# A two-layer decoder trunk: seven products of sums for two of eight pairs of K tiles, with two of the four weight sums made by accumulating DMAs

## The chip, the cores and the metric

One core of a Trainium2 chip runs the whole program. The metric is the device time of one execution in microseconds (us). Engines are named as the profile names them: PE is TensorE (matmul; PEld its weight loads), DVE is VectorE, ACT is ScalarE, POOL is GpSimd, SP is SyncE, which here only issues DMAs. SPq, ACTq and POOLq are these engines as issuers of DMAs.

## What is computed

Two layers over 256 tokens of width 2048, in float32. Nearly all arithmetic is in products of the 256 x K activations with weight matrices:

```python
def swiglu(h, w_gate, w_up, w_down):
    return (jax.nn.silu(h @ w_gate) * (h @ w_up)) @ w_down      # 2048 -> 5632 -> 2048
...
def short_conv_mixer(h, w_in, conv_w, w_out):
    bg, cg, z = jnp.split(h @ w_in, 3, axis=-1)                 # 2048 -> 3 x 2048
    z = cg * z
    zc = lax.conv_general_dilated(z, conv_w[:, None, :], ...)   # depthwise, width 3
    return (bg * zc) @ w_out                                    # 2048 -> 2048
...
def reference(x, ...):
    h = x
    for i in range(DEPTH):                                      # 2
        hn = rmsnorm(h, norm_mix[i])
        if i % 2 == 0:
            mix = sgu_nsa_mixer(hn, ...)                        # 2048 -> 4632 columns, attention, 2048 -> 2048
        else:
            mix = short_conv_mixer(hn, ...)
        h = h + mix
        h = h + swiglu(rmsnorm(h, norm_ffn[i]), w_gate[i], w_up[i], w_down[i])
    return rmsnorm(h, norm_f)
```

## The kernel before

Every product of activations with a weight matrix goes through one object, `Stream`. A weight matrix is cut into strips of 512 columns (NW) and tiles of 128 rows (K tiles). `gemm` plans one strip: a load of four K tiles (1024 KB) at a time on SP's queue into `raw` (three buffers), and units of two K tiles. For a unit, `split` writes each weight as a rounded part `wh` (ScalarE, L82) and the rest `wl` (VectorE, L83), and `multiply` issues twelve matmuls: two K tiles, two halves of the tokens (m), and three products each, xh*wh, xh*wl and xl*wh (L99 to L101). The activations are split the same way into a high and a low part (`a_h`, `a_l` for the normed h, `t_h`, `t_l` for the hidden layer, `y`, `z_h`, `z_l`). One strip gathers in two PSUM banks of `psg` (pool of four).

The order is written out by hand: `run` takes unit after unit; after the matmuls of unit i it splits ahead (`ahead`: AHEAD = 3 units, with a ring of AHEAD + 1 pairs `wh`, `wl`), then calls what is due (`done` at a strip's last unit, and functions hung on later units by `at`). Each engine works its own queue in this order. A raw buffer is loaded again as soon as its last split is recorded.

The feed-forward layer does 11 pairs of strips, gate then up; after each pair g = silu(gate) * up is transposed on TensorE into `t_h`, `t_l`; then w_down in four strips of 44 K tiles, added to h (L276, `norm_from`). The convolution layer does for each of four strips cg, z and bg, and then w_out_c. The attention part of layer 0 (up to about 320 us) and w_out_ab use the same stream. At the start SP loads the first pieces of x (256 KB each) and the first weights in turn (end of `trunk`, L176 and L71).

Of the kernel before, what the change touches and what calls it, by code (L numbers as in the profile page):

```python
# [27 lines left out]
NEG = -1e30  # L28
AHEAD = 3
PROBS, VALUES = 4, 6  # L30


class Stream:


    def __init__(self, nc, raws, parts, psg):
        self.nc, self.raws, self.parts, self.psg = nc, raws, parts, psg
        self.raw_plan, self.units = [], []
        self.raw, self.hl = {}, {}
        self.loaded = self.split_to = 0  # L40
        self.hooks = {}
        self.at_unit = 0

    def gemm(self, w, groups, n0, src, done, tail=0, between=None):
# [3 lines left out]
        for gi, g in enumerate(groups):  # L48
            k0, gk = g if isinstance(g, tuple) else (g, 4)
            ri = len(self.raw_plan)  # L50
            self.raw_plan.append((w[k0 * P:(k0 + gk) * P, n0:n0 + NW].rearrange("(k p) n -> p k n", p=P), gk * NW))
            for j in range(gk // 2):
                self.units.append({
                    "raw": ri, "j": j, "k0": k0 + 2 * j, "src": src, "chunk": chunk, "free": j == gk // 2 - 1,
                    "first": gi == 0 and j == 0, "last": gi == len(groups) - 1 and j == gk // 2 - 1, "tail": 0,
                })
            if between and gi < len(groups) - 1:
                ap, use = between.pop(0)
                self.units.append({"raw": len(self.raw_plan), "j": 0, "use": use, "free": True})
                self.raw_plan.append((ap, 2 * NW))  # L60
        if tail:
            self.units[-tail]["tail"] = tail

# [11 lines left out]
    def split(self, pieces=(slice(0, 2),)):  # L75
        u = self.units[self.split_to]
        nc = self.nc
        src = self.raw[u["raw"]][:, 2 * u["j"]:2 * u["j"] + 2, :]
        hv = self.parts.tile([P, 2, NW], F32R, name="wh")
        lv = self.parts.tile([P, 2, NW], F32R, name="wl")  # L80
        for ks in pieces:
# [889 lines left out]
```

## Time and profile before

| | |
|---|---|
| median of 3 runs | 2187.59 us (2186.87 to 2188.07) |
| profiled execution | 2187.05 us, span 2185.3 us |
| TensorE busy | 2174.6 us |
| VectorE, ScalarE busy | 1149.6 us, 988.3 us |
| moved by DMA | 410.95 MB, mean 188 GB/s |
| granted clock | 0.999 of full speed |

The profile is that of one execution; busy time is the time in which an engine has an instruction, and for TensorE neighbouring matmuls overlap, so the mean of one record is more than the distance between two. The page gives shares over the whole span; stages differ, so the text below reads the feed-forward stage (500 to 1000 us, and again in the second layer) by itself.

### The profile page before, as it was taken

The page shows a single profiled execution, that of the slowest core. Times are in us where ns is not written, and L with a number is a line of the kernel's source. Part 1 is how long each engine was busy: PE and PEld are TensorE (multiplying, and loading weights), DVE is VectorE, ACT ScalarE, POOL GpSimd, SP SyncE. Part 2 cuts the span into 40 slices and gives each one's busy share as a digit, 9 for nine tenths or more (in the row PEclk, how much of TensorE's full clock was granted, in tenths as well). Part 3 has the DMA queues.
Part 4 walks back from the last instruction along what each step waited for, and adds up shares of the span by engine and source line. Part 5 has one row for each costly group of instructions (what it writes and reads, how often), then busy time and mean ns, then how long its engine had stood idle before and what let it go on. Part 6 is the DMA issues. An engine that isn't in the chain of part 4 may idle for free.

```text
span 2185.3 us, 24414 instructions
## 1 busy us (share of the span) xinstructions
PE 2174.6 (100%) x9900; PEld 1796.8 (82%) x9900; DVE 1149.6 (53%) x1269; ACT 988.3 (45%) x1178; POOL 28.3 (1%) x59
## 2 busy tenths in 40 slices
PE   9999999999999999999999999999999999999998
PEld 7887788888888888888888888888888888888886
DVE  6577655555444544544455555554554455444444
ACT  6456545444444444444444444444444444444443
POOL 2000000000000000000000000000000000000000
PEclk9999999999999999999999999999999999999999
DMA  7664455665555555555556555556555555556553
GB/s 261 204 198 134 136 176 190 193 193 183 188 190 191 192 191 188 188 187 190 192 184 201 185 182 191 190 187 192 192 193 191 188 186 186 192 193 197 197 193 135
DMA packets 214577, 410.95 MB, mean 188 GB/s; under 512 B 6744, under 2 KB 18448, under 8 KB 214464
## 3 DMA queue, kind: packets, MB, share of 16 engines
q1 hardware_dynamic: 210416, 404.52, 56.9%
q10 hardware_dynamic: 3664, 3.63, 0.5%
q8 instruction: 77, 1.26, 0.2%
q0 software_dynamic: 384, 1.25, 0.2%
q14 instruction: 36, 0.29, 0.0%
HBM read 407.27 MB, written 2.10 MB: 187 GB/s over the span
## 4 chain that ended last, share of the span: by engine, by line
PE 99%; issue 0%; DMA 0%; DVE 0%; SPq 0%; POOLq 0%; POOL 0%; ACT 0%; DVEq 0%
PE pg L99 32%; PE pg L101 32%; PE pg L100 32%; PE pm L227 2%; PE pm L537 0%; PE pm L614 0%; PE pm L403 0%; PE pm L570 0%; DMA h<-in_x_dram 0%; PE pm L501 0%; PE pm L688 0%; PE pm L617 0%; PE pm L577 0%; POOLq L966 0%; POOL nf_r L899 0%
## 5 line engine op out<-in xcount | busy, mean ns | idle before, releaser
L83 DVE TENSOR_TENSOR wl<-raw,wh 128x1024 fp32r<-128x1024 f32 (+1 forms) x769 | 939.1, 1224 | 923.0 <-ACT wh L82 920.4
L82 ACT ACTIVATE wh<-raw 128x1024 fp32r<-128x1024 f32 (+1 forms) x769 | 812.0, 1059 | 962.3 <-PE pg L101 952.7
L99 PE MATMUL pg<-wh,a_h 128*128 128x512 f32 x2080 | 820.6, 394 | 0.0
L101 PE MATMUL pg<-wh,a_l 128*128 128x512 f32 x2080 | 810.6, 390 | 0.0
L100 PE MATMUL pg<-wl,a_h 128*128 128x512 f32 x2080 | 810.0, 389 | 0.0
L101 PEld LDWEIGHTS pg<-wh,a_l 128*128 128x128 f32 x2080 | 390.7, 188 | 82.1
L100 PEld LDWEIGHTS pg<-wl,a_h 128*128 128x128 f32 x2080 | 391.0, 188 | 81.7 <-issue 2.2
L99 PEld LDWEIGHTS pg<-wh,a_h 128*128 128x128 f32 x2080 | 390.9, 188 | 81.4 <-issue 2.1
L99 PE MATMUL pg<-wh,t_h 128*128 128x512 f32 x704 | 274.3, 390 | 0.0
L101 PE MATMUL pg<-wh,t_l 128*128 128x512 f32 x704 | 273.9, 389 | 0.0
L100 PE MATMUL pg<-wl,t_h 128*128 128x512 f32 x704 | 273.9, 389 | 0.0
L101 PEld LDWEIGHTS pg<-wh,t_l 128*128 128x128 f32 x704 | 132.1, 188 | 27.4
L100 PEld LDWEIGHTS pg<-wl,t_h 128*128 128x128 f32 x704 | 132.2, 188 | 27.3
L99 PEld LDWEIGHTS pg<-wh,t_h 128*128 128x128 f32 x704 | 132.2, 188 | 27.3
L99 PE MATMUL pg<-wh,y 128*128 128x512 f32 x128 | 50.4, 394 | 0.0
L99 PE MATMUL pg<-wh,z_h 128*128 128x512 f32 x128 | 50.2, 392 | 0.0
L101 PE MATMUL pg<-wh,y 128*128 128x512 f32 x128 | 49.9, 390 | 0.0
L101 PE MATMUL pg<-wh,z_l 128*128 128x512 f32 x128 | 49.9, 390 | 0.0
L100 PE MATMUL pg<-wl,y 128*128 128x512 f32 x128 | 49.8, 389 | 0.0
L100 PE MATMUL pg<-wl,z_h 128*128 128x512 f32 x128 | 49.8, 389 | 0.0
L239 DVE TENSOR_TENSOR t_l<-pm,t_h 128x512 fp32r<-128x512 f32 x44 | 28.4, 686 | 32.4 <-ACT t_h L238 32.4
L238 ACT ACTIVATE t_h<-pm 128x512 fp32r<-128x512 f32 x44 | 23.9, 595 | 46.2 <-PE pm L227 46.2
(182 smaller groups left out, 780.3 us busy)
## 6 DMA issues: line engine op xcount, KB each, us to landing
raw<-in_w_gate_dram SPq DMA_DIRECT2D x88, 1024.0 KB, 5.2
raw<-in_w_up_dram SPq DMA_DIRECT2D x88, 1024.0 KB, 5.2
raw<-in_w_down_dram SPq DMA_DIRECT2D x88, 1024.0 KB, 5.1
raw<-in_w_in_c_dram SPq DMA_DIRECT2D x48, 1024.0 KB, 5.1
raw<-in_w_in_ab_dram SPq DMA_DIRECT2D x34, 1024.0 KB, 5.2
raw<-in_w_out_ab_dram SPq DMA_DIRECT2D x16, 1024.0 KB, 5.1
raw<-in_w_out_c_dram SPq DMA_DIRECT2D x16, 1024.0 KB, 5.1
raw<-in_w_in_ab_dram SPq DMA_DIRECT2D x4, 512.0 KB, 6.7
```

The costliest lines, as they stand in the source:

```text
L82: nc.scalar.activation(hv[:, ks], src[:, ks], AF.Copy)
L83: nc.vector.tensor_sub(lv[:, ks], src[:, ks], hv[:, ks].bitcast(F32))
L99: nc.tensor.matmul(ps[m], xh[:, kt, sl], hv[:, k, :], start=u["first"] and k == 0, stop=False)
L100: nc.tensor.matmul(ps[m], xh[:, kt, sl], lv[:, k, :], start=False, stop=False)
L101: nc.tensor.matmul(ps[m], xl[:, kt, sl], hv[:, k, :], start=False, stop=u["last"] and k == 1)
L227: nc.tensor.transpose(t[:, k * S + m * P:k * S + (m + 1) * P], src[:, m, c + k * P:c + (k + 1) * P], ident)
L238: nc.scalar.activation(dh[:, k0:k0 + 2, :], t, AF.Copy)
L239: nc.vector.tensor_sub(dl[:, k0:k0 + 2, :], t, dh[:, k0:k0 + 2, :].bitcast(F32))
```

## The change

The two strips that belong together (gate and up, two strips of w_down, cg and z, two of bg, two of w_out_c) become one `block`. In it a pair of K tiles and the two strips form a product of 2 x 2 tiles: tiles of x for two K tiles and two halves of the tokens, tiles of w for two K tiles and two strips. For most pairs it is done as before, in 8 products of three matmuls each, as units of kind n with twelve matmuls. For the pairs numbered 4 and 6 of eight (`SUMS`; of six pairs only number 4) it is done with seven products of sums of tiles: four differences of x tiles (`x_split`, lines L430 to L432 on VectorE), four sums of w tiles, and sums of the products (`summed`). These take four units of kind s: three with six matmuls, one with three. With a0, a1 the two K tiles of the first strip and b0, b1 of the second, the weight sums are a0 + b0 and b1 + b0 (loads of a0 and b1 into `ts`, and for each a DMA from GpSimd that adds b0 to it, L184), a0 + b0 + b1 and a0 + a1 + b0 + b1 (VectorE, L137 and L140). The strings N8, F8 and N6 set the order of the units: N8 is five n, then s and n mixed, then three n; F8 ends with two n, and so does N6 (six pairs). Four products keep banks of their own (`FREE`, from `psm`, which also serves the transposes); the other four banks (`BANK`) are those of `psg`, and gather ordinary products and three of the seven.

Loads are now of two K tiles (512 KB) into six buffers, eight from the end of w_out_ab on, and from there the ring of split weights has five places, so splits run four units ahead. The feed-forward layer is done in three parts of 4, 4 and 3 strips (`PARTS`): gate/up blocks of a part, then its part of w_down, added to h. The last two strips of w_down in layer 1 stay as they were. The attention part and w_out_ab are as before apart from the size of the loads. At the start SP sends two weight loads where it sent one.

```diff
+RAWS = 6
+MORE = 2
+TS = 2
+PARTS = (4, 4, 3)
+SUMS = {4: 0, 6: 1}
+BANK = ((1, 3), (2, 7))
+P1, P5, P6, P7 = FREE = (0, 4, 5, 6)
...
+    def widen(self, pool):
+
+        self.ring.insert(self.slot, (pool, len(self.ring)))
+        self.sums = pool
+        self.free += [pool] * MORE
...
+            item = queue[c].pop(0)
+            if c == "n":
+                item[1]["raw"] = self.plan(item[0])
+                u = item[1]
+            elif item:
+                wk, t, s = item
+                ts = []
+                ra, rb = self.plan(wk[0]), self.plan((wk, ts))
+                sums13 = None
+
+                def sum2(ra=ra, rb=rb, ts=ts):
+                    self.nc.vector.tensor_add(self.raw[rb][:, 0], ts[0][:, 0], self.raw[rb][:, 1])
+
+                def sum4(ra=ra, rb=rb, ts=ts):
+                    self.nc.vector.tensor_add(ts[0][:, 2], self.raw[rb][:, 0], self.raw[ra][:, 1])
+
+                sevens = [
+                    {"raw": ra, "prep": sums13, "mms": [(0, t(0, 0), P1), (1, t(1, 0), BANK[0][0])]},
+                    {"raw": rb, "ts": ts, "at": 0, "then": sum2, "mms": [(0, s(1), P5), (1, s(0), P7)]},
+                    {"raw": rb, "then": sum4, "frees": (ra,), "mms": [(0, s(2), P6), (1, s(3), BANK[1][0])]},
+                    {"raw": rb, "ts": ts, "at": 2, "w": 1, "mms": [(0, t(1, 1), BANK[0][1])]},
+                ]
+                u = sevens.pop(0)
+            else:
...
+        assert not queue["n"] and not queue["s"]
+        self.on(last_sum, lambda: summed(0, chunk["banks"]))
+        self.on(last_sum + 1, lambda: summed(1, chunk["banks"]))
+        end = len(self.units)
+        self.soon[end - 1] = lambda: done(0, chunk["banks"])
+        self.soon[end] = lambda: done(1, chunk["banks"])
+        for u, fn in begun:
+            self.on(first + u, fn)
...
     def load(self):
-        if self.loaded < len(self.raw_plan):
-            ap, n = self.raw_plan[self.loaded]
-            t = self.raws.tile([P, 4 * NW], F32, name="raw")
-            self.nc.sync.dma_start(out=t[:, :n].rearrange("p (k n) -> p k n", n=ap.shape[-1]), in_=ap)
-            self.raw[self.loaded] = t.rearrange("p (k n) -> p k n", n=NW)
+        while self.free and self.loaded < len(self.raw_plan):
+            ap = self.raw_plan[self.loaded]
+            pool = self.free.pop(0)
+            t = pool.tile([P, 2 * NW], F32, name="raw", bufs=RAWS if pool is self.raws else MORE)
+            v = t.rearrange("p (k n) -> p k n", n=NW)
+            if isinstance(ap, tuple):
+                (wa, wb), ts = ap
+                ts.append(self.sums.tile([P, 3, NW], F32, name="ts", bufs=TS))
+                self.nc.sync.dma_start(out=ts[0][:, 0], in_=wa[:, 0])
+                self.nc.sync.dma_start(out=ts[0][:, 1], in_=wb[:, 1])
+                for k in range(2):
+                    self.nc.gpsimd.dma_start(out=ts[0][:, k], in_=wb[:, 0], accum_op=ALU.add)
+                self.nc.sync.dma_start(out=v[:, 1], in_=wb[:, 1])
+            else:
+                self.nc.sync.dma_start(out=t.rearrange("p (k n) -> p k n", n=ap.shape[-1]), in_=ap)
+            self.raw[self.loaded] = v
+            self.home[self.loaded] = pool
             self.loaded += 1
...
+        for ks in pieces or (slice(0, w),):
             nc.scalar.activation(hv[:, ks], src[:, ks], AF.Copy)
+            if "then" in u:
+                u["then"]()
             nc.vector.tensor_sub(lv[:, ks], src[:, ks], hv[:, ks].bitcast(F32))
-        self.hl[self.split_to] = (hv, lv)
+        self.hl[i] = (hv, lv)
         self.split_to += 1
-        if u["free"]:
-            self.load()
+        if "frees" in u:
+            self.free.append(self.home[u["raw"]])
+            if u["frees"] != 1:
+                self.free.append(self.home[u["frees"][0]])
+        self.load()
...
+        c = u["chunk"]
+        if "mms" in u:
+            for x, (j, op, key) in enumerate(u["mms"]):
+                uses = c["uses"][key]
+                if uses[0] == (i, x):
+                    c["banks"][key] = self.bank(key)
+                ps = c["banks"][key]
+                xh, xl = op()
+                nc.tensor.matmul(ps, xh, hv[:, j, :], start=uses[0] == (i, x), stop=False)
+                nc.tensor.matmul(ps, xh, lv[:, j, :], start=False, stop=False)
+                nc.tensor.matmul(ps, xl, hv[:, j, :], start=False, stop=uses[-1] == (i, x))
+            return
...
-        while self.split_to < min(len(self.units), i + 1 + min(AHEAD, 2 + i // 8)):
+        while self.split_to < min(len(self.units), i + 1 + min(len(self.ring) - 1, 2 + i // 8)):
...
             self.multiply(i)
+            if i in self.soon:
+                self.soon[i]()
             self.ahead(i)
...
+    def x_split(src, dst, kp, gain=None):
+
+        ks = slice(2 * kp, 2 * kp + 2)
+        if kp not in SUMS:
+            split_T([src.rearrange("p (k m) c -> p k (m c)", k=2)], (dst.h, dst.l), 2 * kp, gain)
+            return
+        xs = late["pool"].tile([P, 8, P], F32, name="xs")
...
+        v = a.rearrange("p (k m) c -> p k (m c)", k=2)
+        nc.vector.tensor_sub(xs[:, 4:6], a[:, 0:2], a[:, 1:4:2])
+        nc.vector.tensor_sub(xs[:, 6], a[:, 0], xs[:, 5])
+        nc.vector.tensor_sub(xs[:, 7], a[:, 2], xs[:, 6])
+
+        def parts():
+            i = SUMS[kp]
+            nc.scalar.activation(dst.h[:, ks], v, AF.Copy)
+            nc.scalar.activation(dst.sh[:, i], xs[:, 4:], AF.Copy)
+            nc.vector.tensor_sub(dst.l[:, ks], v, dst.h[:, ks].bitcast(F32))
+            nc.vector.tensor_sub(dst.sl[:, i], xs[:, 4:], dst.sh[:, i].bitcast(F32))
+
+        st.at(1, parts)
...
+    def summed(part, b):
+
+        if part == 0:
+            g, u = (late["pool"].tile([P, MT, NW], F32, name=n) for n in ("ga", "ub"))
+            late["g"], late["u"] = g, u
+            nc.scalar.activation(g[:, 0], b[P1], AF.Copy)
+            return
+        g, u = late["g"], late["u"]
+        nc.vector.tensor_sub(u[:, 0], b[P6], g[:, 0])
+        nc.vector.tensor_sub(g[:, 1], b[P7], u[:, 0])
+        nc.vector.tensor_sub(u[:, 1], b[P5], g[:, 1])
+        nc.vector.tensor_add(u[:, 0], b[P5], u[:, 0])
...
+    def add_to_h(n2, squares=None):
+
+        c0 = 2 * n2 * NW
+
+        def sums(part, b):
+            summed(part, b)
+            if part:
+                for n, t in enumerate((late["g"], late["u"])):
+                    hs = h[:, :, c0 + n * NW:c0 + (n + 1) * NW]
+                    nc.vector.tensor_add(hs, hs, t)
+
+        def done(n, b):
+            for m in range(MT):
+                hs = h[:, m, c0 + n * NW:c0 + (n + 1) * NW]
+                nc.vector.tensor_add(hs, b[BANK[n][m]], hs)
+            if squares:
+                st.at(1, lambda: [squares(2 * n2 + n, m) for m in range(MT)])
+
+        return sums, done
...
+    N8 = [(k, k in SUMS) for k in range(8)], "nnnnn sns sns sns sns nnn"
+    F8 = [(k, k in (4, 6)) for k in range(8)], "nnnnnn sns sns sns sns nn"
+    N6 = [(k, k in SUMS) for k in range(6)], "nnn nn sn sn sn s nn"
...
+                st.block([(w_gate[layer], 0, c * NW), (w_up[layer], 0, c * NW)], F8 if c == 0 else N8, src_a, begun[:],
+                         summed, done)
+                begun[:] = [(2, lambda p=pairs: p(0)), (3, lambda p=pairs: p(1))]
+            last = part == len(PARTS) - 1
+            for n2 in range(2):
+                if last and layer == 1 and n2 == 1:
+                    break
+                sums, done = add_to_h(n2, norm[0] if last else None)
+                ws = [(w_down[layer], 4 * c0, 2 * n2 * NW), (w_down[layer], 4 * c0, (2 * n2 + 1) * NW)]
+                st.block(ws, N8 if nb == 4 else N6, src_x, begun[:], sums, done)
+                begun[:] = norm[1](n2) if last else []
+            c0 += nb
+
+    def then_pairs(pair, scale):
...
+    order = F8
+    for c in (0, 2):
+        for cc in (c, c + 1):
+            done, then = done_cz(cc)
+            st.block([(wc, 0, D + cc * NW), (wc, 0, 2 * D + cc * NW)], order, src_a, begun[:], summed, done)
+            begun[:] = then
+            order = N8
+        done, then = done_bg(c)
+        st.block([(wc, 0, c * NW), (wc, 0, (c + 1) * NW)], N8, src_a, begun[:], summed, done)
+        begun[:] = then
+    squares, pair, scale = norm_from("f1", g_ffn[1])
+    begin = then_pairs(pair, scale)
+    for n2 in range(2):
+        sums, done = add_to_h(n2, squares)
+        st.block([(w_out_c[0], 0, 2 * n2 * NW), (w_out_c[0], 0, (2 * n2 + 1) * NW)], N8 if n2 else F8, src_x, begun[:], sums,
+                 done)
+        begun[:] = begin(n2)
 
 
...
+    free = st.free
     for b in range(3):
+        st.free = free[:2]
         st.load()
```

How the order of instructions moves, at three places. The first is TensorE in a gate/up block. Before, half a unit, one of its two K tiles (with numbers: pg_5360 and pg_5361 are the banks of the two halves of the tokens):

```order
L99 MATMUL pg_5360<-wh_5335,a_h_79 128x512
L100 MATMUL pg_5360<-wl_5336,a_h_79 128x512
L101 MATMUL pg_5360<-wh_5335,a_l_80 128x512
L99 MATMUL pg_5361<-wh_5335,a_h_79 128x512
L100 MATMUL pg_5361<-wl_5336,a_h_79 128x512
L101 MATMUL pg_5361<-wh_5335,a_l_80 128x512
```

Now, the second and third unit of a pair done with sums (sa_h and sa_l are the split sums of x tiles, pm the banks of single products):

```order
L229 MATMUL pm_3767<-wh1_3703,sa_h_2717 128x512
L230 MATMUL pm_3767<-wl1_3704,sa_h_2717 128x512
L231 MATMUL pm_3767<-wh1_3703,sa_l_2718 128x512
L229 MATMUL pm_3771<-wh1_3703,sa_h_2717 128x512
L230 MATMUL pm_3771<-wl1_3704,sa_h_2717 128x512
L231 MATMUL pm_3771<-wh1_3703,sa_l_2718 128x512
L229 MATMUL pm_3779<-wh2_3727,sa_h_2717 128x512
L230 MATMUL pm_3779<-wl2_3728,sa_h_2717 128x512
L231 MATMUL pm_3779<-wh2_3727,sa_l_2718 128x512
L229 MATMUL pg_3646<-wh2_3727,sa_h_2717 128x512
L230 MATMUL pg_3646<-wl2_3728,sa_h_2717 128x512
L231 MATMUL pg_3646<-wh2_3727,sa_l_2718 128x512
```

A split weight now feeds one half of the tokens only, and a unit has six matmuls. Over the program the matmuls of 512 columns in these products are 237 fewer, and the transposes of activations number 368 in both.

The second place is SP's queue in the same blocks: the loads of weights. Before, four of a strip of gate, then four of up:

```order
L71 DMA raw<-in_w_in_ab_dram 128x4x512 x18
L71 DMA raw<-in_w_out_ab_dram 128x4x512 x16
L71 DMA raw<-in_w_gate_dram 128x4x512 x4
L71 DMA raw<-in_w_up_dram 128x4x512 x4
L71 DMA raw<-in_w_gate_dram 128x4x512 x4
```

Now, around the two summed pairs of a block (L181 and L182 load the two tiles of `ts` that GpSimd's DMAs of L184 add to, L185 the second tile of the second strip again):

```order
L187 DMA raw<-in_w_gate_dram 128x2x512 x2
L181 DMA ts<-in_w_gate_dram 128x512
L182 DMA ts<-in_w_up_dram 128x512
L185 DMA raw<-in_w_up_dram 128x512
L187 DMA raw<-in_w_up_dram 128x2x512
L187 DMA raw<-in_w_gate_dram 128x2x512 x2
```

A summed pair takes one load of 512 KB and three of 256 KB here, and two accumulations of 256 KB on GpSimd's queue. There the row scales (`r_f`, `r_c`) stand between accumulations.

The third place is VectorE at the end of a strip of w_down, where its sum goes into h. Before:

```order
L83 TENSOR_TENSOR wl<-raw,wh 128x1024 x21
L276 TENSOR_TENSOR h<-pg,h 128x512 x2
L83 TENSOR_TENSOR wl<-raw,wh 128x1024
L245 SCALAR_TENSOR_TENSOR a_l<-pm,gains,a_h 128x256 x4
L83 TENSOR_TENSOR wl<-raw,wh 128x1024 x21
```

Now, at the end of a block of w_down over six pairs, in layer 0 (ga and ub are the two buffers of product sums; the splits from wl_8689 on belong to the next block):

```order
L208 TENSOR_TENSOR wl_8689<-raw,wh_8688 128x1024
L472 TENSOR_TENSOR ub<-pm,ga 128x512
L473 TENSOR_TENSOR ga<-pm,ub 128x512
L474 TENSOR_TENSOR ub<-pm,ga 128x512
L475 TENSOR_TENSOR ub<-pm,ub 128x512
L503 TENSOR_TENSOR h<-h,ga 128x2x512
L503 TENSOR_TENSOR h<-h,ub 128x2x512
L208 TENSOR_TENSOR wl_8704<-raw,wh_8703 128x1024
L208 TENSOR_TENSOR wl_8722<-raw,wh_8721 128x1024
L508 TENSOR_TENSOR h<-pg,h 128x512 x2
L208 TENSOR_TENSOR wl_8742<-raw,wh_8741 128x1024
L508 TENSOR_TENSOR h<-pg,h 128x512 x2
```

The additions that empty the `pg` banks (L508) stand behind the six operations on product sums and behind three splits for the next block, whose first unit writes into the first of these banks.

## Rows read from the trace of the kernel before

**Rows 1.** The page: busy time, and the span in 40 slices (PE, granted clock, DMA).

```profile
PE 2174.6 (100%) x9900; PEld 1796.8 (82%) x9900; DVE 1149.6 (53%) x1269; ACT 988.3 (45%) x1178; POOL 28.3 (1%) x59
PE   9999999999999999999999999999999999999998
...
PEclk9999999999999999999999999999999999999999
DMA  7664455665555555555556555556555555556553
```

**Rows 2.** The page: the chain that ended last, by engine.

```profile
PE 99%; issue 0%; DMA 0%; DVE 0%; SPq 0%; POOLq 0%; POOL 0%; ACT 0%; DVEq 0%
```

**Rows 3.** Timeline, gate/up stretch of layer 0: start us, us, engine, line, operation [idle before].

```profile
699.83 0.39 PE L99 MATMUL pg<-wh,a_h 128*128 128x512 f32 x1
...
700.51 0.39 PE L99 MATMUL pg<-wh,a_h 128*128 128x512 f32 x1
...
701.39 1.06 ACT L82 ACTIVATE wh<-raw 128x1024 fp32r<-128x1024 f32 x1 [1.66 <-PE pg L101]
...
702.48 1.23 DVE L83 TENSOR_TENSOR wl<-raw,wh 128x1024 fp32r<-128x1024 f32 x1 [1.50 <-ACT wh L82]
...
704.11 1.06 ACT L82 ACTIVATE wh<-raw 128x1024 fp32r<-128x1024 f32 x1 [1.66 <-PE pg L101]
```

**Rows 4.** Chain in order of time: transposes after two successive gate/up pairs (start us, us).

```profile
492.79 0.87 PE pm L227 x8
537.23 0.87 PE pm L227 x8
```

**Rows 5.** Groups of instructions: count | busy us, mean ns of one | idle before.

```profile
L83 DVE TENSOR_TENSOR wl<-raw,wh 128x1024 fp32r<-128x1024 f32 (+1 forms) x769 | 939.1, 1224 | 923.0 <-ACT wh L82 920.4
L82 ACT ACTIVATE wh<-raw 128x1024 fp32r<-128x1024 f32 (+1 forms) x769 | 812.0, 1059 | 962.3 <-PE pg L101 952.7
L769 DVE SCALAR_TENSOR_TENSOR ga<-pg,r_f,ga 128x512 f32<-128x512 f32 x44 | 30.9, 743 | 0.0
L760 ACT ACTIVATE ga<-pg,r_f 128x512 f32<-128x512 f32 x44 | 30.0, 690 | 20.6 <-PE pg L101 20.6
L276 DVE TENSOR_TENSOR h<-pg,h 128x512 f32<-128x512 f32 x24 | 15.4, 682 | 0.0
```

**Rows 6.** Timeline of VectorE in the convolution layer: operations back to back.

```profile
1199.60 1.28 DVE L815 TENSOR_TENSOR cg<-pg,cg 128x512 f32<-128x512 f32 x2
1208.70 3.50 DVE L83 TENSOR_TENSOR wl<-raw,wh 128x1024 fp32r<-128x1024 f32 x3
```

**Rows 7.** Windows: us, busy of PE, PEld, DVE, ACT, POOL, clock, DMA share, GB/s.

```profile
5.00:20.00 15.00, 14.69 (x66) 11.92 (x66) 9.11 (x14) 10.25 (x21) 7.32 (x23) 1.00 1.06 375
500.00:1000.00 500.00, 500.00 (x2248) 414.83 (x2247) 248.27 (x225) 214.66 (x229) 0.00 (x0) 1.00 0.58 190
```

**Rows 8.** DMA issues: count, KB each, median us from issue to landing.

```profile
raw<-in_w_gate_dram SPq DMA_DIRECT2D x88, 1024.0 KB, 5.2
...
raw<-in_w_in_ab_dram SPq DMA_DIRECT2D x4, 512.0 KB, 6.7
...
h<-in_x_dram ACTq DMA_DIRECT2D x5, 256.0 KB, 5.4
nfg<-in_norm_f_dram POOLq DMA_DIRECT2D x4, 256.0 KB, 5.4
```

**Rows 9.** Start: SP's issues on the timeline, and the chain's first piece.

```profile
1.71 0.46 SPq L71 DMA_DIRECT2D raw<-in_w_in_ab_dram  x1
2.21 0.47 SPq L176 DMA_DIRECT2D h<-in_x_dram  x1
...
2.21 4.53 DMA h<-in_x_dram
```

More of the change, by code (lines that the diff above doesn't have):

```diff
@@ L49, in gemm @@
             k0, gk = g if isinstance(g, tuple) else (g, 4)
[L50 to L56, printed above, removed]
+            for k in range(k0, k0 + gk, 2):
+                ri = self.plan(w[k * P:(k + 2) * P, n0:n0 + NW].rearrange("(k p) n -> p k n", p=P))
+                self.units.append({"raw": ri, "k0": k, "src": src, "chunk": chunk, "frees": 1, "first": gi == 0 and k == k0,
+                                   "last": gi == len(groups) - 1 and k == k0 + gk - 2, "tail": 0})
@@ L73, in load, with split @@
             self.loaded += 1
-    def split(self, pieces=(slice(0, 2),)):
-        u = self.units[self.split_to]
+    def split(self, pieces=None):
+        i = self.split_to
+        u = self.units[i]
         nc = self.nc
[L78 to L81, printed above, removed]
+        if u.get("prep"):
+            u["prep"]()
+        w = u.get("w", 2)
+        src = u["ts"][0][:, u["at"]:u["at"] + w] if "ts" in u else self.raw[u["raw"]]
+        pool, k = self.ring[self.slot]
+        self.slot = (self.slot + 1) % len(self.ring)
+        hv = pool.tile([P, 2, NW], F32R, name=f"wh{k}")
+        lv = pool.tile([P, 2, NW], F32R, name=f"wl{k}")
+        for ks in pieces or (slice(0, w),):
@@ L123, in run @@
                 continue
-            if u["first"]:
-                c["ps"] = [self.psg.tile([P, NW], F32, name="pg") for _ in range(MT)]
-            if u["tail"]:
+            if u.get("first"):
+                c["ps"] = [self.bank(k) for k in BANK[self.turn]]
+                self.turn ^= 1
+            if u.get("tail"):
                 for j in range(i, i + u["tail"]):
@@ L266, in trunk @@
     R = {}
[L268 to L290 removed]
+    late = {}
@@ new lines, in x_pair, with open_late @@
+    def x_pair(src, c, dst, kp, gain=None):
+        t = transposed_bank(src, c).rearrange("p k (m c) -> p (k m) c", m=MT)
+        st.at(1, lambda: x_split(t, dst, kp, gain))
+    def open_late():
+        next_region()
+        pool = late["pool"] = region("late")
+        pool.tile([P, LATE_PAD], F32, name="pad")
+        for n in ("a", "x"):
+            for x in "hl":
+                late[n + x] = pool.tile([P, len(SUMS), 4, P], F32R, name=f"s{n}_{x}")
+        src_a.sh, src_a.sl = late["ah"], late["al"]
+        st.widen(pool)
@@ new lines, in second_operand @@
+    def second_operand():
+        src_x.h, src_x.l = (yp.tile([P, KT, S], F32R, name=f"y{i}") for i in range(2))
+        if late:
+            src_x.sh, src_x.sl = late["xh"], late["xl"]
+    def summed(part, b):
[9 more added lines that the diff above has]
+        nc.vector.tensor_add(u[:, 0], b[P5], u[:, 0])
@@ L719, in trunk @@
     st.gemm(win, G4, 512, src_a, done_u(1))
[L721 to L722 removed]
+    on = st.on
     for u in range(6):
@@ L833, in done_bg @@
[L833 to L847 removed]
+                open_late()
```

362 lines of the change are left out of this document (213 added, 149 removed).

## The prediction

> **What bounds the kernel now.** I read the busy shares first. TensorE is busy 2174.6 us of a 2185.3 us span, VectorE 53%, ScalarE 45%, the DMA engines 5 to 6 tenths, and the granted clock is 9 tenths or more (its upper level, 2.4 GHz) in every slice [rows 1]. The chain of waits says the same: 99% of it is TensorE [rows 2]. So nothing is bought on another engine; only a TensorE instruction removed is time gained, for as long as the others deliver. The timeline of a feed-forward stretch gives the price. Three matmuls of 512 columns follow each other in 0.68 us (from 699.83 to 700.51), 0.2267 us each; the 0.39 us of one record overlaps the next. A unit of twelve takes 2.72 us, seen in ScalarE's starts at 701.39 and 704.11, and VectorE waits 1.50 us for ScalarE's part before each of its splits: both helpers follow TensorE [rows 3]. A gate and up pair takes 44.44 us from one group of transposes to the next, 537.23 less 492.79 [rows 4], which is 192 x 0.2267 = 43.5 us and 0.87 us of transposes.
>
> **What the change removes.** A block is a pair of weight column strips with its eight (or six) pairs of K tiles. A pair done the old way is 8 products, 24 matmuls; done with sums it is 7, 21 matmuls. The blocks count as 22 gate/up, 8 down of eight pairs, 3 down of six, 8 in the convolution layer: 41. Two pairs each, one in the six-pair blocks: 38 x 2 + 3 = 79 pairs. So 237 matmuls go, 237 x 0.2267 = 53.7 us, and a gate/up block should take 43.1 us. The transposes stay as many (368 before and after, by the order), and no TensorE instruction is added.
>
> **What it adds, and what hides it.** *VectorE.* A gate/up block has 18 splits of 1024 columns (1.224 us), 16 operations of 512 (0.682 us) and 2 at 0.743 us [rows 5]: 22.0 + 10.9 + 1.5 = 34.4 us of 43.1. It was 22.4 of 44.4. This is hidden by TensorE's 43.1 us, with 8.7 us left; where that is gone, each us over is a us of the block. ScalarE has 18 x 1.059 us and seven smaller ones of about 0.69, some 24 us: hidden. Sums of activations fall on 22 of the pairs written, about 1.5 us of VectorE each, in blocks that have the 8.7 us: nothing.
>
> *The turn of a block.* The four banks that collect ordinary products serve the next block at once, so the first bank must be emptied before TensorE's next first unit. In VectorE's queue the emptying stands behind the sums of product banks. Take as zero the end of the last unit that feeds those banks. Back to back, VectorE takes 1.28 us for two operations of 512 and 3.50 us for three splits [rows 6], so 0.60 and 1.14 us per operation, 0.68 where one needs the last. In a block that adds to h, the queue is one split (ends at 2.2 to 2.5), four sums (5.0 to 5.3), two additions of 1024 columns (1.14 each, 7.3 to 7.5), two or three splits, one addition of 0.60. In the four blocks with two units at the end (three six-pair blocks and the first output block of the convolution layer) the bank is free at 10.1, while TensorE arrives after 2.72 + 0.68 + 2.72 + 2.72 = 8.84 us: 1.3 us late, four times 1.3 = 5.2 us. In the nine with three units at the end it is free at about 11.7, TensorE arrives at 11.56: 0.2 us, 1.8 us in all. In the other 28 blocks the 2.3 us of additions are missing and the bank is free about 2 us before it is needed: nothing.
>
> *Transfers.* Loads of 1024 KB become 512 KB; a summed pair takes 512 KB, three of 256 KB and two accumulations of 256 KB. A block of eight pairs moves 9.5 MiB (9.96 MB) where it moved 8 MiB. In the start-up stretch from 5 to 20 us, 256 and 512 KB transfers together ran at 375 GB/s with the engines full, while the feed-forward stretch uses 190 GB/s and 0.58 of them [rows 7]. At 375 GB/s a block needs 26.6 us, and 29.4 us with each accumulation counted twice, of 43.1: hidden. The Trainium skill, "DMA: Bandwidth & Descriptors" (Rules for kernel authors; the fit in Anatomy of one DMA), speaks against this: full rate wants 1 MiB per transfer, and one costs 2.0 us plus its bytes at 436 GB/s. By its fit, one transfer after another, the block's 14 of 512 KB and 10 of 256 KB would take about 71 us (an estimate), and the time would be near 3280 us; the start-up rows show such transfers overlapping, and by them the term is nothing.
>
> *The accumulations.* The trace of before has none. The nearest row is a 256 KB load issued by GpSimd, 5.4 us from issue to landing; that is the lower bound and the value I take [rows 8]. Upper bound: what the lookahead bears. Splits run four units ahead of TensorE. The load of a summed pair can go out once unit 18 of the block before is split, and ScalarE wants the sum for the split of unit 7. In between TensorE does seven units of 2.72 and one of 0.68, 19.7 us, less 2.2 us for the split that frees the slot: 17.5 us. TensorE comes to unit 7 itself 9.5 us later, of which 2.9 us go to ScalarE, the sum and the split. That makes 24 us before TensorE stands still. The plain loads take up to 5.4 us (256 KB of x) [rows 8], so the two accumulations may take 18.6 us, over three times the row. On GpSimd's queue only the row scales stand behind a waiting accumulation; they are wanted a block later: nothing. On SP, eight loads in 44 us become twenty at some 0.47 us of issue [rows 9]: nothing.
>
> *Start.* SP now sends two 512 KB weight loads ahead of the second piece of x, where one stood. The chain begins with that piece, landing 4.53 us after 2.21 us [rows 9]. 524 KB at 375 GB/s is 1.4 us. Lower bound nothing (the engines had room before 5 us), upper bound two such loads, 2.8 us.
>
> **The sum.** The profiled execution took 2187.05 us. Less 53.7, plus 5.2, 1.8 and 1.4, is 2141.75 us. The median shown is 0.54 us above that execution, so I forecast **2142 us**, 2.1% faster. About 0.2%, 4.4 us, is what a measurement of this kernel can tell from no change.
>
> **Rivals.**
> *VectorE becomes the bound (12%).* If the four dependent sums cost more than I took, or splits wait at the turn for ScalarE, the other 28 blocks lose their 2 us of room. 1.3 us in each of the 41 blocks is 53 us and eats the gain; 0.5 us more in each gives 2163. For it: 34.4 of 43.1 us, in order, with waits on TensorE and ScalarE between. Against: every split now starts with 1.50 us of waiting [rows 3], so the queue has room where no bank is emptied. Range 2152 to 2187; a third of this case lies within 0.2% of before.
>
> *The accumulations come late (slower, 10%).* Point of decision: a pair of accumulations over 18.6 us. VectorE then stands at the first sum, with splits behind it, and TensorE runs out of units. If each took 10.8 us, twice the row, and the second began when the first had landed, load and pair take 27.0 us, 3 us over; 41 blocks x 3 = 123 us, 2265. It undoes the gain from 1.3 us over. Against: the two write different rows and wait for different loads, so nothing in the order makes one wait for the other. For: no row shows one. The Trainium skill, "Collectives: The Full Stack" (The bandwidth ceiling), says an add inside a DMA engine needs two source reads and ran at about half a copy's rate; that is the doubling taken here, and no run here shows it.
>
> *No lateness at all (10%).* The turns and the start cost nothing: 2134.
>
> That the products don't go away is excluded: the order counts 237 fewer.
>
> **How the numbers follow.** My own sum holds 68%, 2136 to 2152 by its bounds (start 0 to 2.8, the turns from nothing to twice 7 us). Faster by over 0.2%: 68 + 10 + 8 of the first rival = 86%. Within 0.2%: 4%. Slower: 10%. The range runs from 2133 to 2168: it takes in my case, no lateness and the nearer half of the first rival, about 84%.
>
> **What would show it.** Right: 237 matmuls fewer at the same 0.2267 us; transposes of gate/up blocks 43.1 us apart; VectorE near 80% in feed-forward; idle time of about 1.3 us on TensorE at the turns of the six-pair blocks and none in the gate/up blocks; accumulations landing within about 6 us. Wrong: TensorE waiting on a split whose ScalarE or VectorE part waits for a sum tile's DMA, a DMA share near 1, or gate/up blocks of 44 us and more.

## The result, and the profile after

The median went from 2187.38 to **2150.74 us** (four runs each; the changed kernel's lay between 2150.60 and 2150.82): a ratio of 0.9832, with a 95% interval of 0.9815 to 0.9849. The forecast was 2142 us, with a range of 2133 to 2168. Direction and range held; the forecast was 8.7 us too fast. The profiled execution took 2150.60 us, with a span of 2148.9.

The page's busy shares after the change, engine by engine (busy us, share of the span, instructions):

```profile
PE 2128.4 (99%) x9663; PEld 1750.3 (81%) x9663; DVE 1610.4 (75%) x1981; ACT 1146.3 (53%) x1411; POOL 161.0 (7%) x217
```

Against [rows 1], TensorE has 237 matmuls fewer, as counted, and is still the engine that is always busy; VectorE has gone from 53% to 75%. The chain of waits at the transposes of two successive gate/up blocks (start, duration, what):

```profile
498.46 0.44 PE pm L370 x4
...
541.58 0.44 PE pm L370 x4
```

One block takes 43.12 us (541.58 less 498.46), where it took 44.44 [rows 4]. The forecast was 43.1. The window of the feed-forward stretch (columns as in [rows 7]), and two kinds of DMA issue (count, KB each, median us from issue to landing) with the queues' shares of the 16 engines:

```profile
500.00:1000.00 500.00, 500.00 (x2231) 412.71 (x2230) 385.21 (x428) 260.43 (x285) 39.77 (x46) 1.00 0.77 232
```

```profile
ts<-in_w_up_dram POOLq DMA_DIRECT2D x88, 256.0 KB, 5.7
ts<-in_w_down_dram POOLq DMA_DIRECT2D x38, 256.0 KB, 6.7
...
q1 hardware_dynamic: 229104, 425.27, 60.4%
q0 software_dynamic: 23136, 42.67, 12.1%
```

VectorE is busy 77% of that stretch and TensorE all of it. The accumulations, which no row of before showed, land 5.7 and 6.7 us after their issue. Where TensorE did wait for something is one short list:

```profile
PE pg L229 <- DVE h L508: 4.7, 3, 1.6
PE pm L370 <- DMA h<-in_x_dram: 1.7, 1, 1.7
PE pg L238 <- DVE h L508: 1.6, 1, 1.6
...
PE pg L239 <- DVE wl L208: 0.8, 1, 0.8
PE pg L238 <- ACT wh L205: 0.6, 1, 0.6
...
```

Each line gives the waiting group, its releaser, us in total, times, and the longest. Two things stand out. The first is four waits for VectorE's L508, the emptying of a bank into h: 6.3 us, in exactly the four blocks of the forecast, 1.57 us each. The other is the waits at the start for x, for `wh` and for `wl`. The first compression matmul (L501 before, L721 after), which comes behind the start-up, moved from 59.45 to 63.88 us. On the chain its first group of eight stands here, before and after:

```profile
59.62 0.94 PE pm L501 x8
...
64.04 0.94 PE pm L721 x8
```

So **the start lost 4.4 us**, where 1.4 was forecast. That is one execution: in the profiles of the five trials below that leave this start as it is, the same matmul begins between 63.42 and 65.36 us. ScalarE's timeline there shows the place (start, duration, engine, line; in brackets the idle time before and what ended it):

```profile
5.99 0.44 ACTq L319 DMA_DIRECT2D h<-in_x_dram  x1
...
...
7.67 5.78 ACTq L319 DMA_DIRECT2D h<-in_x_dram  x4
13.50 0.84 ACT L386 ACTIVATE a_h<-pm,gains 128x256 fp32r<-128x256 f32 x2 [5.83 <-DMA h<-in_x_dram]
```

The same place before:

```profile
7.09 1.58 ACTq L176 DMA_DIRECT2D h<-in_x_dram  x3
8.72 0.84 ACT L243 ACTIVATE a_h<-pm,gains 128x256 fp32r<-128x256 f32 x2 [1.18 <-DMA raw<-in_w_in_ab_dram]
```

ScalarE issues five late pieces of x itself. Before, the last three issues took 1.58 us; now four of them take 5.78, and the part of x that it should round next (its transposes start at 8.36 us) waits until 13.50. The list of ScalarE's instructions with their waits says why. After the change:

```
L319 DMA h<-in_x_dram 128x2x256
L319 DMA h<-in_x_dram 128x2x256 [waits DMAHW3_49]
L319 DMA h<-in_x_dram 128x2x256 [waits DMAHW5_49]
L319 DMA h<-in_x_dram 128x2x256 [waits DMAHW6_49]
L319 DMA h<-in_x_dram 128x2x256 [waits DMAHW7_49]
L386 ACTIVATE a_h<-pm,gains 128x256 [waits PE_49]
```

In these lists the DMAs of SP and ScalarE share eight completion semaphores, DMAHW0 to 7 (_49 is a suffix that the program gives all its semaphores), and an issue that takes a used one waits for the transfer it stood for. With six buffers instead of three, SP's weight loads run ahead and take semaphores first, so four issues of x wait for transfers under way. Before, three of them waited (on numbers 0, 3 and 4), for transfers nearly or long done. The chain goes through it, from the third piece of x to ScalarE's queue:

```profile
4.48 8.58 DMA h<-in_x_dram
...
13.08 0.37 ACTq L319
...
13.50 0.84 ACT a_h L386 x2
```

### The profile page after: what moved, and what is told of

Read it like the earlier page. It is cut to its first block, busy times and chain, and to the rows that moved or that the text cites. A ratio compares the mean times of both kernels' runs of the same rounds, so it can differ in the third digit from the quotient of the medians.

```text
span 2148.9 us, 27123 instructions
## 1 busy us (share of the span) xinstructions
PE 2128.4 (99%) x9663; PEld 1750.3 (81%) x9663; DVE 1610.4 (75%) x1981; ACT 1146.3 (53%) x1411; POOL 161.0 (7%) x217
## 3 DMA queue, kind: packets, MB, share of 16 engines
q1 hardware_dynamic: 229104, 425.27, 60.4%
q0 software_dynamic: 23136, 42.67, 12.1%
q8 instruction: 76, 1.25, 0.2%
## 4 chain that ended last, share of the span: by engine, by line
PE 96%; DVE 1%; issue 1%; DMA 1%; ACT 1%; SPq 0%; POOLq 0%; POOL 0%; DVEq 0%; ACTq 0%
PE pg L229 23%; PE pg L231 22%; PE pg L230 22%; PE pg L238 5%; PE pg L240 5%; PE pg L239 5%; PE pm L231 3%; PE pm L229 3%; PE pm L230 3%; PE pm L370 2%; DVE wl L208 1%; PE pm L757 0%; PE pm L834 0%; DMA h<-in_x_dram 0%; PE pm L623 0%
## 5 line engine op out<-in xcount | busy, mean ns | idle before, releaser
L229 PE MATMUL pg<-wh,a_h 128*128 128x512 f32 x1456 | 572.1, 393 | 1.6 <-DVE h L508 1.6
L231 PE MATMUL pg<-wh,a_l 128*128 128x512 f32 x1456 | 567.4, 390 | 0.0
L230 PE MATMUL pg<-wl,a_h 128*128 128x512 f32 x1456 | 566.8, 389 | 0.0
L229 PEld LDWEIGHTS pg<-wh,a_h 128*128 128x128 f32 x1456 | 273.4, 188 | 58.9 <-ACT wh L205 2.0
L229 PE MATMUL pg<-wh,y 128*128 128x512 f32 x646 | 253.8, 393 | 3.1 <-DVE h L508 3.1
L231 PE MATMUL pg<-wh,y 128*128 128x512 f32 x646 | 251.7, 390 | 0.0
L230 PE MATMUL pg<-wl,y 128*128 128x512 f32 x646 | 251.4, 389 | 0.0
L205 ACT ACTIVATE wh<-ts 128x1024 fp32r<-128x1024 f32 (+1 forms) x158 | 133.8, 847 | 92.2 <-PE pg L231 91.0
L208 DVE TENSOR_TENSOR wl<-ts,wh 128x1024 fp32r<-128x1024 f32 (+1 forms) x158 | 150.6, 953 | 35.6 <-ACT wh L205 35.6
L184 POOL DMA_DIRECT2D ts<-in_w_up_dram x88 | 76.3, 1015 | 947.0 <-DVE ub L475 324.3
L229 PEld LDWEIGHTS pg<-wh,y 128*128 128x128 f32 x646 | 121.3, 188 | 29.7 <-ACT wh L205 3.9
L231 PEld LDWEIGHTS pg<-wh,y 128*128 128x128 f32 x646 | 121.2, 188 | 25.7
L230 PEld LDWEIGHTS pg<-wl,y 128*128 128x128 f32 x646 | 121.4, 188 | 24.6
L238 PE MATMUL pg<-wh,a_h 128*128 128x512 f32 x288 | 121.0, 420 | 0.6 <-ACT wh L205 0.6
L239 PE MATMUL pg<-wl,a_h 128*128 128x512 f32 x288 | 113.1, 393 | 0.8 <-DVE wl L208 0.8
L240 PE MATMUL pg<-wh,a_l 128*128 128x512 f32 x288 | 113.4, 394 | 0.0
L238 PE MATMUL pg<-wh,y 128*128 128x512 f32 x176 | 69.1, 393 | 1.6 <-DVE h L508 1.6
L240 PE MATMUL pg<-wh,y 128*128 128x512 f32 x176 | 68.5, 389 | 0.0
```

The source lines that it names most:

```text
L184: self.nc.gpsimd.dma_start(out=ts[0][:, k], in_=wb[:, 0], accum_op=ALU.add)
L205: nc.scalar.activation(hv[:, ks], src[:, ks], AF.Copy)
L208: nc.vector.tensor_sub(lv[:, ks], src[:, ks], hv[:, ks].bitcast(F32))
L229: nc.tensor.matmul(ps, xh, hv[:, j, :], start=uses[0] == (i, x), stop=False)
L230: nc.tensor.matmul(ps, xh, lv[:, j, :], start=False, stop=False)
L231: nc.tensor.matmul(ps, xl, hv[:, j, :], start=False, stop=uses[-1] == (i, x))
```

## The experiments

The theories after this reading: (1) the 237 matmuls give 53.7 us; (2) the start loses 4.4 us, part by the second piece of x behind two weight loads, part by ScalarE held in its own DMA issues; (3) the turns of the blocks that add to h lose some 8 us because two additions of 1024 columns stand ahead of the emptying; (4) the accumulations cost nothing. The rivals are that (4) hides a cost, that VectorE's load is what is felt, and that the structure costs more than the sums save. Every trial starts from the changed kernel and is compared with its 2150.74 us.

**One weight load per round at the start.**

```diff
-        st.free = free[:2]
+        st.free = free[:1]
         st.load()
...
+    st.free = free[:3]
     x_tiles(1)
```

> Only the start differs from the changed kernel: one 512 KB weight load per round of the start loop as in the kernel before, the other three buffers given out after the loads of x. Theory (the second load in each round delays the second piece of x by 1.6 us, leaves TensorE at its slow pitch for longer, and makes ScalarE stand 5.8 us in its queue of loads): the whole start loss returns, 4.1 to 4.4 us, so about 2146.5 us against 2150.7, and ScalarE issues its five loads without a long stand. Rival (only the transfer time of the second load is in front, as predicted): 1.4 us, 2149.3.

Measured: 2152.07 us (2150.20 to 2152.77), no gain. TensorE's and ScalarE's timelines:

```profile
7.48 6.16 ACTq L319 DMA_DIRECT2D h<-in_x_dram  x4
7.50 0.66 PE L370 MATMUL pm<-ident,h 128*128 128x128 f32 x4 [1.16 <-DMA h<-in_x_dram]
...
15.52 0.50 PE L238 MATMUL pg<-wh,a_h 128*128 128x512 f32 x1 [4.04 <-ACT wh L205]
```

The second piece of x does come earlier (transposed at 7.50 instead of 8.36 us), but the ScalarE stand stays (6.16 us; its issues have the same four waits, since SP's next loads still find free buffers and go ahead of them). TensorE only reaches the same wait sooner and stands 4.04 us. After that, in the window 16 to 24 us, the granted clock is 0.79:

```profile
16.00:24.00 8.00, 7.24 (x29) 5.82 (x29) 4.92 (x8) 5.10 (x11) 0.00 (x0) 0.79 0.92 322
```

Some matmuls there follow each other in 0.43 us instead of 0.23: the lower of the two levels, 1.2 GHz, for part of the stretch. The edit alone does not bring this about, for two trials below that leave the start as it is (late additions, no sums) have a clock of 0.79 in the same window. The first of them:

```profile
16.00:24.00 8.00, 7.53 (x29) 6.03 (x30) 4.70 (x8) 4.79 (x11) 0.00 (x0) 0.79 0.92 326
```

Both theories of this trial fell: neither all of the loss nor 1.4 us hung on the second load alone.

**The late pieces of x on SP.**

```diff
     for c in range(3, 8):
-        x_load(nc.scalar, c)
+        x_load(nc.sync, c)
```

> Only the five late loads of x (256 KB) are issued by SP instead of ScalarE; the second weight load of each round stays. Theory (of the 4.4 us at the start some 1.8 come from ScalarE standing behind issues that wait for earlier transfers, the other 2.6 from the second piece of x landing 1.6 us later and from 1.0 us of slow matmuls): 1.5 to 2 us faster than the changed kernel, 2149, with a_h of the second group at about 9.2 us instead of 13.5. Rival (ScalarE's stand hides behind the late piece of x): no difference. Second rival: x pieces 3 to 7 now come later, as SP itself waits, and TensorE waits for them: slower than 2150.7.

Measured: 2148.30 us (2148.12 to 2149.12), 2.4 us faster. ScalarE rounds the second group at 9.02 us and no longer stands in issues; what is left is TensorE's wait for x:

```profile
8.25 0.73 PE L370 MATMUL pm<-ident,h 128*128 128x128 f32 x4 [2.29 <-DMA h<-in_x_dram]
...
16.99 0.63 PE L370 MATMUL pm<-ident,h 128*128 128x128 f32 x4 [0.56 <-DMA h<-in_x_dram]
```

The first wait is for the second piece of x, as in the changed kernel; the second for a later piece, which SP now issues behind weight loads. So the two paths run side by side, and mending one shows the other.

**Both: SP issues x and weights in turn.**

```diff
-    for b in range(3):
-        st.free = free[:2]
+    for b in range(6):
+        st.free = free[:1]
         st.load()
-        if b < 2:
-            x_load(nc.sync, b + 1)
+        x_load(nc.sync, b + 1)
+    x_load(nc.sync, 7)
...
-    for c in range(3, 8):
-        x_load(nc.scalar, c)
```

> Only the start differs from the changed kernel: SP alone issues all pieces of x and the first six weight loads in turn, one of each, and ScalarE issues none. New theory after the first two starts (two paths end at the same place: ScalarE held by issues that wait for earlier transfers until 13.5 us, and the second piece of x behind two weight loads; each kept the loss alone, and every idle time of TensorE there adds slow matmuls behind it): with both gone the first matmuls of the compression (59.45 us before, 63.88 changed, 65.44 and 61.68 in the two trials) come at 59.5 to 60.5, and the time falls by 3.5 to 4.4 us, to 2146.5 to 2147.3. Rival (the third or a later piece of x is late whatever the order, as the 0.56 us wait in the second trial): about 2148.3, as that trial.

Measured: 2145.88 us (2145.61 to 2146.44), 4.9 us faster, a little more than expected. The compression's first matmul is at 59.08 us, 0.37 earlier than before the change.

```profile
6.84 0.93 PE L370 MATMUL pm<-ident,h 128*128 128x128 f32 x4 [0.37 <-DMA h<-in_x_dram]
```

This is all that TensorE's list of waits still holds for x or weights at the start. The start term was 4.9 us by the runs (0.4 of it gained on the kernel before), and it belongs to the order of issues, not to the bytes.

**The two wide additions after the emptying.**

```diff
         def sums(part, b):
             summed(part, b)
-            if part:
-                for n, t in enumerate((late["g"], late["u"])):
-                    hs = h[:, :, c0 + n * NW:c0 + (n + 1) * NW]
-                    nc.vector.tensor_add(hs, hs, t)
...
         def done(n, b):
             for m in range(MT):
...
+            t = (late["g"], late["u"])[n]
+            def later():
+                hs = h[:, :, c0 + n * NW:c0 + (n + 1) * NW]
+                nc.vector.tensor_add(hs, hs, t)
...
+            st.at(1, later)
```

> In the blocks that add to h the two additions of 1024 columns (gathered sums into h) come one unit after the emptying of the banks instead of ahead of it. Theory (these 2.3 us stand between the last sum and the first emptied bank): the four stalls of 1.57 us at six-pair turns and at the first output block go (6.3 us), and up to 0.2 us in each of nine others: 6 to 8 us faster, 2143 to 2145. Rival (the chain of four sums and the splits, not the additions, set when the bank is free): under 2 us.

Measured: 2142.07 us (2141.48 to 2143.17), 8.7 us faster. VectorE's timeline at the first six-pair turn of the changed kernel, to see what was moved:

```profile
1033.88 0.68 DVE L475 TENSOR_TENSOR ub<-pm,ub 128x512 f32<-128x512 f32 x1
1034.48 1.21 DVE L503 TENSOR_TENSOR h<-h,ga 128x1024 f32<-128x1024 f32 x1
1035.61 1.22 DVE L503 TENSOR_TENSOR h<-h,ub 128x1024 f32<-128x1024 f32 x1
1036.75 2.35 DVE L208 TENSOR_TENSOR wl<-raw,wh 128x1024 fp32r<-128x1024 f32 x2
1039.02 1.28 DVE L508 TENSOR_TENSOR h<-pg,h 128x512 f32<-128x512 f32 x2
```

and of this trial:

```profile
1034.22 0.68 DVE L475 TENSOR_TENSOR ub<-pm,ub 128x512 f32<-128x512 f32 x1
1034.82 2.35 DVE L208 TENSOR_TENSOR wl<-raw,wh 128x1024 fp32r<-128x1024 f32 x2
1037.09 1.28 DVE L504 TENSOR_TENSOR h<-pg,h 128x512 f32<-128x512 f32 x2
```

From the last sum to the emptying it is 5.14 us in the first and 2.87 in the second: the 2.3 us of additions. All four waits for a bank are gone from TensorE's list; those give 6.3 us. The nine other blocks that add to h give most of the rest: at each of their nine turns the chain of the changed kernel has one matmul of 0.45 or 0.46 us where the others have 0.23, and in this trial it has none; nine times 0.23 is 2.1 us.

**No accumulations.**

```diff
-                for k in range(2):
-                    self.nc.gpsimd.dma_start(out=ts[0][:, k], in_=wb[:, 0], accum_op=ALU.add)
```

> Leaves out the accumulating DMAs (line 184), so the weight sums a0 + b0 and b1 + b0 are not made and the result of these products differs; all else stands. Theory (accumulations are hidden): the same time within 0.1%, 2149 to 2152. Rival (some of the 4 us over the sum that no wait of TensorE explains comes from their traffic or from late sum tiles): 2 to 4 us faster.

Measured: 2150.36 us (2149.92 to 2151.65): no difference. The share of the transfer engines in the window 410 to 1000 us falls from 0.78 to 0.65, and no wait of TensorE goes. As they stand, the accumulations cost no time.

**Sums by VectorE instead.**

```diff
-                self.nc.sync.dma_start(out=ts[0][:, 0], in_=wa[:, 0])
-                self.nc.sync.dma_start(out=ts[0][:, 1], in_=wb[:, 1])
-                for k in range(2):
-                    self.nc.gpsimd.dma_start(out=ts[0][:, k], in_=wb[:, 0], accum_op=ALU.add)
-                self.nc.sync.dma_start(out=v[:, 1], in_=wb[:, 1])
+                self.nc.sync.dma_start(out=v, in_=wb)
...
-                sums13 = None
+                def sums13(ra=ra, rb=rb, ts=ts):
+                    self.nc.vector.tensor_add(ts[0][:, 0], self.raw[ra][:, 0], self.raw[rb][:, 0])
+                    self.nc.vector.tensor_add(ts[0][:, 1], self.raw[rb][:, 1], self.raw[rb][:, 0])
```

> The two accumulating DMAs are replaced by two more additions of 128 x 1024 values in total per pair on VectorE (two of 512 columns), with both 512 KB loads whole. Theory (accumulations and VectorE are both hidden in the middle of a block): VectorE goes from about 77% to about 84% of a feed-forward stretch, and the time stays within 2 us of 2150.7. Rival (VectorE's room is used up: the additions push the last sums and the emptied banks at each turn): 1.4 us in some 28 blocks and more, 2170 to 2200, with TensorE waiting for VectorE at gate/up turns. If it is faster than 2149, the accumulations did cost something.

Measured: 2150.27 us (2149.93 to 2150.97): no difference. The feed-forward window:

```profile
500.00:1000.00 500.00, 500.00 (x2231) 412.79 (x2230) 412.69 (x474) 260.53 (x285) 0.00 (x0) 1.00 0.62 197
```

VectorE is now at 83% and TensorE still never waits in this stretch. The accumulating DMAs take 27.5 us of VectorE's work out of this window (412.69 less 385.21) for 35 GB/s more of transfers, and since neither is the bound, they neither gain nor lose. This also fells the first rival of the prediction: VectorE had room for more than the forecast load.

**Each accumulation twice.**

```diff
-                for k in range(2):
+                for k in (0, 1) * 2:
```

> Each of the two accumulations is issued twice (the sums become a0 + 2 b0 and b1 + 2 b0, so the result of these products differs); the second one on the same rows waits for the first. Theory (a pair of accumulations may take 18.6 us before TensorE waits): two in a row take 11 to 14 us, the time stays within 1 us of 2150.7, DMA share in feed-forward near 0.9. Rival (the room is smaller, or the shared transfer engines are at their limit): TensorE waits for splits of the sum tiles, 1 us and more in each of 41 blocks, 2190 or slower.

The sums of weights hold one more b0 each. Measured: 2159.02 us (2158.70 to 2167.51), 8.3 us slower; both theories missed. The profile is of the slowest execution (2167.51 us; the other three lie between 2158.70 and 2159.08), so its waits are more than the median lost. From 330 to 1000 us TensorE waits nowhere in it, so the feed-forward part of layer 0 bears the second accumulations. The loss begins in the convolution layer. The chain there, through one pair of sums, and TensorE's waits from 1120 to 1420 us:

```profile
1151.35 6.13 DMA ts<-in_w_in_c_dram
...
1158.04 7.03 DMA ts<-in_w_in_c_dram
...
1167.60 6.55 DMA ts<-in_w_in_c_dram
...
1174.26 1.07 ACT wh L205
```

```profile
PE pm L229 <- DVE zc L1074: 3.2, 3, 2.1
PE pm L229 <- ACT y L436: 2.9, 1, 2.9
PE pm L231 <- DVE y L438: 2.6, 1, 2.6
```

From the first accumulation to the split it is 16.2 us (1158.04 to 1174.26), within the 18.6 us that the prediction allowed, and TensorE has units enough. But the split that waits holds ScalarE and VectorE, and behind it in their queues stand the convolution (`zc`) and the rounding of the next operand (`y`), which TensorE does wait for. Its longest wait for `zc`, 2.06 us at 1316.69, stands behind a pair of 17.6 us (1289.96 to 1307.58), also within the 18.6. Behind some of these waits the matmuls follow in 0.43 us for a while (granted clock 0.57 from 1366 to 1373 us, where the changed kernel has 1.00). How the 8.3 us of the median divide among these is not shown. The room was reckoned for the weights alone.

**No sums at all, the structure kept.**

```diff
-SUMS = {4: 0, 6: 1}
+SUMS = {}
...
-    N8 = [(k, k in SUMS) for k in range(8)], "nnnnn sns sns sns sns nnn"
+    N8 = [(k, k in SUMS) for k in range(8)], "n" * 16
...
-                        nc.vector.tensor_add(t, b[BANK[n][m]], t)
+                        nc.vector.tensor_copy(t, b[BANK[n][m]])
```

(F8 and N6 likewise, and no call of `summed`.)

> All structure stays (blocks, loads of 512 KB, eight raw buffers, five places for split weights, the new start), but every pair is done in eight products: no sums of x or w tiles, no gathered sums, no accumulations; the 237 matmuls come back. Theory (the 237 matmuls are worth 53.7 us, the turns cost 6.3 to 8.7 us, the start 4.4, the rest of the structure nothing): 2150.7 + 53.7 - 6.3 to 8.7 = 2195.7 to 2198.1 without further room. Rival (the structure itself, without sums, costs nothing but the start, and some other part of the sums costs the remaining 2 to 4 us): 2187.4 + 4.4 = 2191.8. Second rival (a removed matmul is not worth 0.2267 us): well below 2190.

Measured: 2194.86 us (2193.11 to 2196.31), between the two expectations. Two of its gate/up blocks on the chain:

```profile
459.35 0.44 PE pm L368 x4
...
503.84 0.44 PE pm L368 x4
```

They are 44.49 us apart with the same 192 matmuls that took 44.44 before: the transposes come in two groups of four instead of eight together, which is the only difference seen on the chain; the block is 0.05 us longer. From 44.49 to 43.12 the sums save 1.37 us a block for six matmuls, 0.228 each. In its profile the compression's first matmul is at 65.18, 5.7 us later than before, and the span 7.2 longer; the structure behind the start therefore costs about 1.5 us. A removed matmul of a gate/up block is worth what the prediction said.

**Both mends, with either way of making the sums.** The diffs are those above, together.

> Both mends together: at the start SP alone issues x and the first weights in turn, and in the blocks that add to h the two wide additions come after the emptying of the banks. Theory (two separate losses, 4.9 us at the start and 8.7 us at the turns): they add up, 2150.7 - 4.9 - 8.7 = 2137.1, between 2136 and 2139. Rival (the removed loss at one place is met again at the other, or a third bound shows): 2141 or more.

> The same two mends, and the sums a0 + b0 and b1 + b0 made by VectorE instead of accumulating DMAs. Theory (either way of making the sums is hidden): the same time as the run with both mends, within 1 us, with VectorE near 83% of a feed-forward stretch and some 62 MB less to move. Rival (with the turns shortened, VectorE's queue now decides): 2 us or more slower than that run.

Measured: **2137.52 us** (2136.70 to 2138.30; ratio to the kernel before 0.9772, interval 0.9758 to 0.9785) with the accumulations, **2136.87** (2136.13 to 2137.16; 0.9769, 0.9755 to 0.9782) with VectorE's sums. The two losses add up (2137.1 expected), the accumulations again make no difference that these runs can tell, and both kernels beat the one before and the changed one. All that TensorE still waits for in the first of them:

```profile
PE pm L1211 <- POOL mhalf L324: 1.4, 1, 1.4
PE pm L370 <- DMA h<-in_x_dram: 0.9, 1, 0.9
PE pm L370 <- DVE h L509: 0.4, 2, 0.2
PE pm L231 <- DVE y L438: 0.3, 1, 0.3
PE pm L1211 <- DVE gains L1215: 0.3, 1, 0.3
```

## Why the prediction was right, and where it was off

*The matmuls.* Right: 237 are gone, and the block of 43.12 us and 0.228 us a matmul in the trial without sums bear out the price for the 132 of them that stood in gate/up blocks. For the rest it is taken over.

*VectorE and ScalarE hidden.* Right. VectorE is at 77% of a feed-forward stretch (near 80% was said), gate/up turns show no wait, and it bears 83% as well. The rival "VectorE becomes the bound" needed waits there; there are none.

*The turns.* The mechanism and the four blocks were right, the size somewhat low: 1.57 us each where 1.3 was reckoned, 0.23 where 0.2 was, and 8.7 us together by the trial with the late additions where 7.0 stood in the sum.

*The transfers.* Right: the feed-forward stretch moves 232 GB/s with a share of 0.77, and TensorE waits for none of it. The Trainium skill's fit, "DMA: Bandwidth & Descriptors" (Anatomy of one DMA), is measured there on single transfers issued by GpSimd. Summed over the block's transfers it gave the estimate near 3280 us; the 2150.74 us measured, with transfers that overlap, do not follow it.

*The accumulations.* Right: leaving them out changes nothing. Per MB they take 0.284% of the engines' span (12.1% for 42.67 MB) against 0.142% for ordinary loads (60.4% for 425.27 MB), twice as much. This agrees with the Trainium skill, "Collectives: The Full Stack" (The bandwidth ceiling), where an add's two source reads halve the rate. GpSimd's queue by itself is not the reason: in the trial without accumulations its plain loads took 0.2% (rounded) for 1.25 MB, 0.12 to 0.2% per MB. The doubling is real, but in engine time, which was free; the landing time is only 0.3 and 1.3 us over the 5.4 that was taken. The rival that they come late had the wrong place of decision: in the trial with each accumulation twice, with pairs of 16.2 and 17.6 us, under the 18.6 allowed, the median lost 8.3 us. The one profile, of a slower execution, shows TensorE waiting for other work queued behind the waiting splits.

*The start.* **This is the step that failed.** It read "SP now sends two 512 KB weight loads ahead of the second piece of x" and took 1.4 us, with 2.8 as the upper bound; it measured 4.4 us in the profile and 4.9 in the runs. The late piece of x alone was roughly priced: its transposes start 1.58 us later (8.36 instead of 6.78). What the step left out was the other queue. ScalarE issues five DMAs ahead of its own work, the waits on completion semaphores changed when SP got more buffers, and 5.8 us of standing followed. The instruction order of before and after, with the waits, showed this without a run; the prediction looked at the order for TensorE and VectorE only. Slow matmuls are not what cost the time in this execution: they follow in 0.43 us until 13.54 us (the clock column shows 1.00 there), before only until 9.93, but TensorE then waits for ScalarE's `wh` all the same. In the trial with VectorE's sums, whose start is the same, they follow in 0.23 us from 11.45 us on; TensorE waits 1.6 us for `wh` instead of 0.6, and the compression begins at 64.10 us, no earlier.

*The sum.* The forecast's misses are 1.7 us at the turns and 3.5 at the start; the structure behind the start, a term that the sum did not have, adds about 1.5 by the trial without sums. Together 6.7 of the 8.7 us. The rest, some 2 us, stays open: the one wait of 0.3 us for y is all of it that the profile names, and nothing was tried to separate more. That the time stayed within the sum's own bounds (2136 to 2152) is in part luck: the start went beyond its upper bound of 2.8 us, and the wide bound on the turns covered it.

## What to carry to other kernels

Where a change gives one queue more buffers, look at every engine that issues DMAs: its issues may now wait for completions of transfers that are none of its own, and its computing stands behind them. Reckon a turn from the last sum to the first emptied bank in the queue's own order, and put what nobody waits for behind the emptying. A tolerance for a late operand holds only if nothing else is queued behind the instruction that waits for it.

## What was not expected of the hardware

A mend of one of two paths can gain nothing: with one weight load per round the end of TensorE's first unit came 3.2 us earlier in the profile (the next transposes start at 10.89 instead of 14.13), its successor was not ready, and TensorE idled for 4.04 us; the run was no faster. The matmuls after that followed in 0.43 us instead of 0.23, with a granted clock of 0.79 in the window, but that varies by itself: of the six profiled kernels with the changed kernel's own start, two show the same stretch. And an accumulating DMA of 256 KB lands almost as soon as a plain load of that size (medians of 5.7 to 6.8 us against 5.1 to 6.9 for the plain loads into the same tiles), though it takes twice the engine time per byte.
